# Two mixing layers: the spatial mixer's projection is issued between the differential heads' projection and their turning

## The chip, the cores and the metric

The kernel runs on one core of one Trainium2 chip. The metric is the device time of one launch in microseconds (us). Engines are named as in the profile: PE is TensorE (PEld its weight loads), DVE is VectorE, ACT is ScalarE, POOL is GpSimd, SP is the engine that here only issues DMAs. Each engine takes its instructions strictly in the order in which they were queued.

## The reference, cut to what matters

Two blocks on a sequence of 256 rows of 1024 values: first a block with a gated delta rule, latent attention and two SwiGLU layers, then a second block with two layers `l`. Only the second block is touched. In each of its layers four mixers run on the same normed `h` and their 256-wide results are put side by side:

```
pa, pb, pc, pd = split(h @ w_in[l], GROUP_COLS)
ya = rwkv7_mixer(pa, ...)            # a scan over the rows, chunked
yb = diff_attention_mixer(pb, ...)   # q, k: norm per head, rotary turn; two softmaxes
yc = spatial_gating_mixer(pc, ...)   # u, v = split(gelu(pc)); v = layer_norm(v); u * (w @ v + b)
yd = forgetting_attention(pd, ...)   # q, k: norm per head; softmax with a decay
x = x + g1 * (concat(ya, yb, yc, yd) @ w_out[l])
```

All matrices are f32. A product of f32 accuracy is made of three matmuls of a 32-bit form whose operands are a high part and a low remainder: high by high, low by high, high by low.

## The kernel before, in words

`mix2` (L1424) is one mixing layer; it runs twice, near 790 to 965 us and near 1182 to 1365 us of the profiled span. The 256 rows are two halves `t` of 128 rows.

**Weights.** `weights` (L446) loads one chunk of weights by a DMA on SP into one of three raw slots, casts it to its high part on ACT (L464) and takes the low remainder on POOL (L467) or on DVE (L469). Which of the two is said by the letter, P or V, at the chunk's running number in the string `w` of the stage's plan (L68 to L98). The high and low parts go to one of three slots (`WSB`); a slot is free again when the last matmul that reads it is done. A chunk of `w_b` or `w_d` has 768 columns, one of `w_c` or `w_out` has 1024.

**The parts.** `mix2` names its parts by letters and `order` lists them. `b2+L` weaves two parts, two steps of the first to one of the second; what stands after `/` runs once the tiles for the result exist.

- B, `diff_heads` (L1899): projection of the differential heads (`proj_qkv`, L1874, 8 chunks, 96 matmuls into two PSUM banks `ps_qk` and one `ps_v`), then, for each half `t`, the turning: squares on ACT, a norm on DVE (`head_scale`), the rotary turn of q on DVE and of k on POOL (L1937 to L1943, six products each), four transposes on PE (L1947), and copies to `at_q` and `b_kbd` on ACT and DVE (L1949 to L1955).
- V, `rwkv_values`; L, `rwkv_levels`; S, `rwkv_scan`; s, `rwkv_out`: the scan mixer. V is a chain over PE, ACT and POOL; L joins the inverse of 32-row blocks that `tri_inverse` (L1858) makes on DVE; S walks over the two chunks of 128 rows.
- M, `forget_gates`; D, `forget_heads` (8 chunks, 96 matmuls, then the norm of the heads and transposes); d, `forget_attend`.
- b, `diff_attend`; e, `diff_out`.
- C, `spatial_in` (L2143): 4 chunks, 48 matmuls of 512 columns into two PSUM banks `ps_c`, for each chunk first one half and then the other; then for each half Gelu on ACT straight from PSUM (L2161, L2164) and the layer norm (L2165 to L2174). c, `spatial_out`, uses it.

Before the change the order is `B V M b2+L D+S C / e s d c`. Last comes `proj_out`, the output projection `ps_o`.

**What sets the order on an engine.** The order in the source is a priority, not the queue: a planner walks through the program in a modelled time and gives each engine the earliest listed instruction whose inputs the model holds ready. So a late part's work is found early in the trace wherever its inputs are there and an engine was modelled idle, and a matmul of a later projection stands between the links of an earlier chain. Tiles of one tag share a fixed number of buffers: tag `acc` (the projections) has 4 PSUM banks, tags `mm` and `A` (the small products) 2 each. `issue_after` puts a block's instructions behind a given instruction on that engine.

Of the kernel before, what the change touches and what calls it, by code (L numbers as in the profile page):

```python
# [11 lines left out]
F32 = mybir.dt.float32  # L12
F32R = mybir.dt.float32r
I32 = mybir.dt.int32
AF = mybir.ActivationFunctionType
# [5 lines left out]
D = 1024  # L21
S = 256
# [4 lines left out]
CW = 1024  # L27
# [25 lines left out]
        w='PPVVVPVVPPPPVPPVPVVVVPVVVP',  # L53
# [14 lines left out]
    m0=dict(  # L68
        np=80,
        w='PPPVVPPPVPPPPVPPPVVPPVPPVVVVPVVVVPP',  # L70
        order='B V M b2+L D+S C / e s d c',
        out=(2, 3, 0, 1, 6, 7, 4, 5),
        hold=4,
        nb=(0,),
# [10 lines left out]
    m1=dict(  # L85
        np=60,
        w='PPPPPPPPPPPVVPVPPVVVVVVVVVVPVVVVVVP',
        order='B V M b2+L D+S C / e s d c',
        out=(2, 3, 0, 1, 6, 7, 4, 5),
        hold=4,  # L90
        nb=(0, 1),
# [288 lines left out]
class Prog:  # L380
# [105 lines left out]
    def mm3_b(self, ps, lhs, w, sl, start, stop, shared=False):  # L486

        nc = self.nc
        wh, wl = w
        xh, xl = lhs  # L490
        kw = dict(skip_group_check=True) if shared else {}
        nc.tensor.matmul(ps, xh, wh[:, sl], start=start, stop=False, **kw)  # L492
        nc.tensor.matmul(ps, xl, wh[:, sl], start=False, stop=False, **kw)  # L493
        nc.tensor.matmul(ps, xh, wl[:, sl], start=False, stop=stop, **kw)  # L494

    def rsqrt(self, out, src, shape, scale, eps, pool=None, tag=None, bufs=1, key=""):

# [926 lines left out]
    def mix2(self, x, l):  # L1424
        nc, tc, ap = self.nc, self.tc, self.ap
        self.lay = self.xp.tile([128, LAYER.n], F32, name=f"lay{l}", tag="lay")
        with tc.issue_after(self.last_raw.ins):
            nc.sync.dma_start(self.lay, ap[f"layer{l}"])
        with ExitStack() as st:
            self.psum(st, 2)  # L1430
            self.rows = self.next_mod
            self.prefetch(*((ap[f"w_k{l}"][c], 776) for c in range(3)))
            self.mq = st.enter_context(tc.tile_pool(name=f"mixq{l}", bufs=1, reuse_waits="tile"))
            xn = [self.mq.tile([128, D], F32, name="xn", tag="b_p", bufs=2) for _ in range(2)]
            sp = self.mq.tile([128, 2, CW], F32R, name="w_sp", tag="b_kbd")
            self.spare = [lambda: (sp[:, 0], sp[:, 1])]
            mp = st.enter_context(tc.tile_pool(name=f"mix{l}", bufs=1, reuse_waits="tile"))
            dr = st.enter_context(tc.tile_pool(name=f"mixd{l}", bufs=1, space=DRAM))
            hl, norm = self.norm_steps(x, True, lambda t: xn[t])
            gate = self.gate_row(2, mp)  # L1440
            A = self.rwkv_scores(l, hl, norm, mp, dr)
            B, C, Dd = {}, {}, {}
            G = dict(B=lambda: self.diff_heads(l, hl, mp, B), C=lambda: self.spatial_in(l, hl, mp, C), D=lambda: self.forget_heads(l, hl, mp, Dd), M=lambda: self.forget_gates(mp, dr, A["f"], Dd, A["last_exp"]),
                     V=lambda: self.rwkv_values(mp, A), L=lambda: self.rwkv_levels(mp, A), S=lambda: self.rwkv_scan(l, mp, A), s=lambda: self.rwkv_out(mp, A, yh, yl),
                     b=lambda: self.diff_attend(l, mp, B), e=lambda: self.diff_out(mp, B, yh, yl), c=lambda: self.spatial_out(l, mp, C, yh, yl), d=lambda: self.forget_attend(l, mp, Dd))
# [451 lines left out]
    def diff_heads(self, l, hl, mp, res):  # L1897
# [21 lines left out]
                V.tensor_tensor(tab[:, t, i], gn[:, :, g], cs[:, c, t].unsqueeze(1).to_broadcast([128, 2, 16]), op=ALU.mult)  # L1919
        ps, pv = yield from self.proj_qkv(hl, ap[f"w_b{l}"])  # L1920
        v = mp.tile([128, 2, 256], F32, name="at_v", tag="at_v", bufs=2)
        qT = mp.tile([128, 2, S], F32, name="at_q", tag="at_q", bufs=2)
        for t in range(2):
            if t == 0:
                nc.scalar.copy(v, pv)
            xn = mp.tile([128, 16, 32], F32, name="b_xn", tag="b_xn", bufs=2)
            rs = self.head_scale(xn, ps[t], 16, 32, 1e-6)
            pv4 = ps[t].rearrange("p (q h d) -> p q h d", q=2, h=8)
# [14 lines left out]
                E.tensor_tensor(ro[:, q, :, 1], ro[:, q, :, 1], m, op=ALU.add)  # L1943
            rf = ro.rearrange("p q h s f -> p (q h s f)")
            pt = self.pm.tile([128, 4, 128], F32, name="ps_qk", tag="mm")
            for j in range(4):
                nc.tensor.transpose(pt[:, j], rf[:, j * 128 : j * 128 + 128], self.ident)  # L1947
            tk = slice(t * 128, t * 128 + 128)
            nc.scalar.copy(qT[:, :, tk], pt[:, 0:2])  # L1949
            for q in range(4):  # L1950
# [6 lines left out]
        res.update(v=v, qT=qT, kbd=kbd, nlam=nlam)  # L1957

    def diff_attend(self, l, mp, a):
        nc = self.nc  # L1960
# [182 lines left out]
    def spatial_in(self, l, hl, mp, res):  # L2143
# [3 lines left out]
        nc.sync.dma_start(sw, ap[f"sgw{l}"])  # L2147
        nc.gpsimd.affine_select(sw, sw, [[0, 4], [1, 128]], ALU.is_ge, 0.0, base=0, channel_multiplier=-1)
        ps = [self.pa.tile([128, 512], F32, name="ps_c", tag="acc") for _ in range(2)]
        for k in range(8):  # L2150
            if k % 2 == 0:
                w = self.weights(ap[f"w_c{l}"][k // 2], CW)
            for t in range(2):
                tk = slice(t * 128, t * 128 + 128)
                self.mm3_b(ps[t], (hl[0][:, k, tk], hl[1][:, k, tk]), w, slice(512 * (k % 2), 512 * (k % 2) + 512), k == 0, k == 7)
            if k % 2:
                yield
        u = mp.tile([128, 2, 256], F32, name="c_u")
        vn = mp.tile([128, 4, 2, 64], F32, name="c_v")
        for t in range(2):  # L2160
            nc.scalar.activation(u[:, t], ps[t][:, 0:256], AF.Gelu)  # L2161
            v = mp.tile([128, 256], F32, name="c_v0", tag="c_v0", bufs=2)
            s = self.sm.tile([128, 2], F32, name="c_s", tag="c_s")
            nc.scalar.activation(v, ps[t][:, 256:512], AF.Gelu, accum_out=s[:, 0:1])  # L2164
            V.tensor_scalar(s[:, 0:1], s[:, 0:1], 1.0 / 256, None, op0=ALU.mult)  # L2165
            V.tensor_scalar(v, v, s[:, 0:1], None, op0=ALU.subtract)
            v2 = mp.tile([128, 256], F32, name="c_v2", tag="c_v0", bufs=2)
# [7 lines left out]
        res.update(sw=sw, u=u, vn=vn)  # L2175

    def spatial_out(self, l, mp, a, yh, yl):
        nc = self.nc
# [93 lines left out]
```

## Time and profile before

| | us |
|---|---|
| three timed runs | 1557.66, 1558.67, 1561.19 (median 1558.67) |
| the profiled execution | 1570.74 |
| its span, first to last instruction | 1569.0 |
| PE busy in the span | 1455.1 (93%) |
| DVE busy | 1120.2 (71%) |
| ACT busy | 811.7 (52%) |
| POOL busy | 659.3 (42%) |
| granted PE clock, mean of the span | 0.972 of full |

Busy time of PE is that of pipelined matmuls, so a PE that is busy all the time need not be at its peak. An idle time in brackets stands ahead of the instruction that ended it, with what it had waited for. A granted clock of 1.00 in a stretch is 2.4 GHz, of 0.50 it is 1.2 GHz.

### The profile page before, as it was taken

The numbers are of one execution on the slowest core, as the hardware profiler recorded it, in microseconds if no ns is written. First come the engines' busy times: TensorE is split into PE (matmuls) and PEld (weight loads), VectorE is DVE, ScalarE is ACT, GpSimd is POOL, SyncE is SP. The second block draws the span as 40 slices with busy tenths as digits, with TensorE's granted clock in tenths as the row PEclk, the third lists the DMA queues.
The fourth block names the chain that finished last, engine by engine and source line by source line (L and its number), as shares of the span: only waits on it lengthen the run. The fifth ranks groups of instructions, "written<-read, shape, count | busy, mean of one in ns | idle before, by whom it ended". The sixth has DMA issues, their size and how long they took to land. (4 is left out here: it accounts for less than half of the span.)

```text
span 1569.0 us, 25783 instructions
## 1 busy us (share of the span) xinstructions
PE 1455.1 (93%) x9586; PEld 1286.3 (82%) x9586; DVE 1120.2 (71%) x2352; ACT 811.7 (52%) x1474; POOL 659.3 (42%) x433
## 2 busy tenths in 40 slices
PE   5999989899999899999988988998998899899998
PEld 4998878699988788999877766898987776589987
DVE  3588668778686577887477597788876768766752
ACT  4676545544543464554354665455544465466651
POOL 3577623256452522443136312465644622236530
PEclk9999999999999999999998999999999999999999
DMA  4756622677884455988434325576773442465551
GB/s 159 232 167 189 182 69 68 209 289 281 298 306 131 136 182 188 337 313 311 170 115 128 108 78 184 203 285 252 264 247 126 120 130 72 141 202 180 191 188 38
DMA packets 103246, 292.96 MB, mean 187 GB/s; under 512 B 28072, under 2 KB 37968, under 8 KB 96976
## 3 DMA queue, kind: packets, MB, share of 16 engines
q1 hardware_dynamic: 93872, 237.12, 44.9%
q10 hardware_dynamic: 8896, 53.14, 9.2%
q8 instruction: 75, 1.23, 0.3%
q0 software_dynamic: 352, 1.06, 0.2%
q14 instruction: 51, 0.42, 0.1%
HBM read 288.04 MB, written 3.24 MB: 186 GB/s over the span
## 5 line engine op out<-in xcount | busy, mean ns | idle before, releaser
L467 POOL TENSOR_TENSOR wl<-raw,wh 128x1024 fp32r<-128x1024 f32 (+4 forms) x162 | 405.6, 2511 | 414.6 <-ACT wh L464 350.7
L464 ACT CAST wh<-raw 128x1024 fp32r<-128x1024 f32 (+3 forms) x421 | 424.1, 1018 | 249.1 <-PE ps_o L493 97.4
L469 DVE TENSOR_TENSOR wl<-raw,wh 128x1024 fp32r<-128x1024 f32 (+2 forms) x259 | 356.9, 1385 | 145.2 <-ACT wh L464 143.2
L480 PE MATMUL ps_gu<-h_hi,wh 128*128 128x256 f32 x1280 | 313.1, 283 | 6.9 <-DVE gu_u L2226 6.3
L480 PE MATMUL ps_gu<-h_lo,wh 128*128 128x256 f32 x1280 | 312.7, 283 | 0.0
L480 PEld LDWEIGHTS ps_gu<-h_hi,wh 128*128 128x128 f32 x1280 | 244.9, 191 | 7.6 <-issue 6.7
L480 PEld LDWEIGHTS ps_gu<-h_lo,wh 128*128 128x128 f32 x1280 | 245.0, 191 | 0.1
L1394 DVE CUSTOM_DVE_ANT_0 ada_raw<-ada_raw,ada_cond 128x1024 f32<-128x1024 f32 x96 | 160.5, 1685 | 68.7 <-DMA ada_raw<-in_ada 68.7
L483 PE MATMUL ps_gu<-h_hi,wl 128*128 128x256 f32 x1280 | 179.2, 283 | 5.9 <-DVE wl L469 3.9
L483 PEld LDWEIGHTS ps_gu<-h_hi,wl 128*128 128x128 f32 x1280 | 164.4, 192 | 6.5 <-DVE wl L469 4.1
L494 PE MATMUL ps_o<-wl,act_h 128*128 128x512 f32 x352 | 138.8, 394 | 0.0
L493 PE MATMUL ps_o<-wh,act_l 128*128 128x512 f32 x352 | 138.6, 394 | 0.0
L492 PE MATMUL ps_o<-wh,act_h 128*128 128x512 f32 x352 | 138.3, 393 | 0.0
L2226 DVE SCALAR_TENSOR_TENSOR gu_u<-ps_gu,f2s,gu_u 128x254 f32<-128x254 f32 (+1 forms) x176 | 82.0, 477 | 40.7 <-ACT gu_u L2224 38.6
L738 POOL TENSOR_TENSOR act_l<-gu_t,act_h 128x256 fp32r<-128x256 f32 x44 | 51.8, 1179 | 102.7 <-ACT act_h L737 102.7
L2229 POOL TENSOR_TENSOR gu_t<-gu_t,gu_u 128x256 f32<-128x256 f32 x44 | 47.4, 1078 | 97.4 <-DVE gu_u L2226 84.1
L494 PEld LDWEIGHTS ps_o<-wl,act_h 128*128 128x128 f32 x352 | 66.1, 188 | 15.4 <-issue 0.5
L493 PEld LDWEIGHTS ps_o<-wh,act_l 128*128 128x128 f32 x352 | 66.1, 188 | 15.1 <-issue 0.2
L492 PEld LDWEIGHTS ps_o<-wh,act_h 128*128 128x128 f32 x352 | 66.1, 188 | 15.0 <-issue 0.2
L737 ACT CAST act_h<-gu_t 128x256 fp32r<-128x256 f32 x44 | 17.7, 407 | 95.8 <-DVE gu_t L736 95.8
L480 PE MATMUL ps_g<-h_hi,wh 128*128 128x256 f32 x256 | 66.5, 294 | 0.0
L480 PE MATMUL ps_g<-h_lo,wh 128*128 128x256 f32 x256 | 66.2, 293 | 0.0
(662 smaller groups left out, 2978.1 us busy)
## 6 DMA issues: line engine op xcount, KB each, us to landing
ada_raw<-in_ada ACTq DMA_DIRECT2D x48, 1024.0 KB, 6.2
raw<-in_f_gu SPq DMA_DIRECT2D x88, 512.0 KB, 5.4
raw<-in_u_gu SPq DMA_DIRECT2D x88, 512.0 KB, 4.2
raw<-in_f_dn SPq DMA_DIRECT2D x44, 512.0 KB, 6.2
raw<-in_u_dn SPq DMA_DIRECT2D x44, 512.0 KB, 4.3
raw<-in_g_qkv SPq DMA_DIRECT2D x32, 512.0 KB, 3.5
raw<-in_g_z SPq DMA_DIRECT2D x16, 512.0 KB, 5.7
raw<-in_g_out SPq DMA_DIRECT2D x16, 512.0 KB, 3.7
```

Source lines behind the costliest of these rows:

```text
L464: self.last_copy = nc.scalar.copy(wh[:, :cols], raw[:, :cols])
L467: nc.gpsimd.tensor_tensor(wl[:, :cols], raw[:, :cols], wh[:, :cols].bitcast(F32), op=ALU.subtract)
L469: nc.vector.tensor_tensor(wl[:, :cols], raw[:, :cols], wh[:, :cols].bitcast(F32), op=ALU.subtract)
L480: nc.tensor.matmul(ps, wh[:, k * width + m0 : k * width + m0 + m], xx[:, k, :], start=(n == 0), stop=(n == last))
L483: self.last_mm = nc.tensor.matmul(ps, wl[:, k * width + m0 : k * width + m0 + m], xh[:, k, :], start=False, stop=(n == last))
L492: nc.tensor.matmul(ps, xh, wh[:, sl], start=start, stop=False, **kw)
L493: nc.tensor.matmul(ps, xl, wh[:, sl], start=False, stop=False, **kw)
L494: nc.tensor.matmul(ps, xh, wl[:, sl], start=False, stop=stop, **kw)
L738: nc.gpsimd.tensor_tensor(al[:, m, :], t, ah[:, m, :].bitcast(F32), op=ALU.subtract)
L1394: nc.vector.tensor_tensor_reduce(raw[:, j], raw[:, j], self.cond, 1.0, 0.0, op0=ALU.mult, op1=ALU.add, accum_out=mod[:, i : i + 1])
L2226: nc.vector.scalar_tensor_tensor(u[:, j, d:], ps[:, j, : S - d], cw[:, 3 * q + 2 - d : 3 * q + 3 - d], u[:, j, d:], op0=ALU.mult, op1=ALU.add)
L2229: nc.gpsimd.tensor_tensor(t, t, u[:, 0], op=ALU.mult)
```

## The change

The letter H is new: `diff_turn` holds the turning that was the second half of B. The letter G is new: `spatial_gelu` holds the Gelu and the layer norm that were the end of C. The order becomes `B C H V M b2+L D+S G / e s d c` in both layers. In C the 48 matmuls go by pairs of chunks: two chunks are held, and each half runs its 24 matmuls of the pair in one go of 12 and 12. At the end of C four copies on ACT take the projection out of PSUM, to `c_u` and `c_v0`; Gelu then works in SBUF, in place. The transposes of the turning are put behind the last matmul of C by `issue_after`. The strings of letters stay, so C's chunks now take the numbers 16 to 19 and D's the numbers 20 to 27 (before: 24 to 27 and 16 to 23). In the first layer those letters are `PVVPPVPP` and `VVVV`, in the second `PVVVVVVV` and `VVVP`.

```diff
-        order='B V M b2+L D+S C / e s d c',
+        order='B C H V M b2+L D+S G / e s d c',          # in m0 and in m1
...
-        nc.tensor.matmul(ps, xh, wl[:, sl], start=False, stop=stop, **kw)
+        self.last_mm = nc.tensor.matmul(ps, xh, wl[:, sl], start=False, stop=stop, **kw)
...
+            G = dict(H=lambda: self.diff_turn(l, mp, B, C), G=lambda: self.spatial_gelu(mp, C), ...
...
         ps, pv = yield from self.proj_qkv(hl, ap[f"w_b{l}"])
         v = mp.tile([128, 2, 256], F32, name="at_v", tag="at_v", bufs=2)
+        nc.scalar.copy(v, pv)
+        res.update(v=v, kbd=kbd, nlam=nlam, tab=tab, ps=ps)
+
+    def diff_turn(self, l, mp, res, behind):
...
         for t in range(2):
-            if t == 0:
-                nc.scalar.copy(v, pv)
...
-            for j in range(4):
-                nc.tensor.transpose(pt[:, j], rf[:, j * 128 : j * 128 + 128], self.ident)
+            with self.tc.issue_after(behind["mm"].ins):
+                for j in range(4):
+                    nc.tensor.transpose(pt[:, j], rf[:, j * 128 : j * 128 + 128], self.ident)
...
-        for k in range(8):
-            if k % 2 == 0:
-                w = self.weights(ap[f"w_c{l}"][k // 2], CW)
+        for c in range(0, 4, 2):
+            w = [self.weights(ap[f"w_c{l}"][c + i], CW) for i in range(2)]
             for t in range(2):
                 tk = slice(t * 128, t * 128 + 128)
-                self.mm3_b(ps[t], (hl[0][:, k, tk], hl[1][:, k, tk]), w, slice(512 * (k % 2), 512 * (k % 2) + 512), k == 0, k == 7)
-            if k % 2:
-                yield
+                for k in range(2 * c, 2 * c + 4):
+                    self.mm3_b(ps[t], (hl[0][:, k, tk], hl[1][:, k, tk]), w[k // 2 - c], slice(512 * (k % 2), 512 * (k % 2) + 512), k == 0, k == 7)
+            yield
         u = mp.tile([128, 2, 256], F32, name="c_u")
+        v = [mp.tile([128, 256], F32, name="c_v0", tag="c_v0", bufs=3) for _ in range(2)]
+        for t in range(2):
+            nc.scalar.copy(v[t], ps[t][:, 256:512])
+            nc.scalar.copy(u[:, t], ps[t][:, 0:256])
+        res.update(mm=self.last_mm, sw=sw, u=u, v=v)
+
+    def spatial_gelu(self, mp, res):
...
-            nc.scalar.activation(u[:, t], ps[t][:, 0:256], AF.Gelu)
+            nc.scalar.activation(u[:, t], u[:, t], AF.Gelu)
...
-            nc.scalar.activation(v, ps[t][:, 256:512], AF.Gelu, accum_out=s[:, 0:1])
+            nc.scalar.activation(v, v, AF.Gelu, accum_out=s[:, 0:1])
```

## Rows read from the trace of the kernel before

**Rows 1.** Stretches: from:to, length, busy PE PEld DVE ACT POOL, clock, DMA
```profile
851.60:866.40 14.80, 11.14 (x49) 8.73 (x48) 13.43 (x75) 5.23 (x9) 7.98 (x14) 0.77 0.24 77
866.40:887.80 21.40, 20.47 (x115) 15.14 (x114) 8.71 (x21) 11.75 (x25) 10.03 (x15) 1.00 0.57 172
908.00:919.30 11.30, 11.30 (x73) 9.10 (x72) 11.04 (x44) 6.98 (x19) 2.27 (x2) 1.00 0.15 49
1245.10:1258.70 13.60, 9.98 (x48) 7.96 (x47) 13.51 (x75) 5.23 (x9) 5.25 (x12) 0.87 0.29 86
```
**Rows 2.** Timeline of PE around the turning: start, length, what, idle before
```profile
858.98 1.13 PE L1947 MATMUL ps_qk<-ident,b_ro 128*128 128x128 f32 x4 [3.59 <-DVE b_ro L1943]
866.88 0.60 PE L1661 MATMUL ps_vt<-ident,a_v 128*128 128x128 f32 x4
1252.49 0.89 PE L1947 MATMUL ps_qk<-ident,b_ro 128*128 128x128 f32 x4 [3.61 <-DVE b_ro L1943]
1259.17 0.60 PE L1661 MATMUL ps_vt<-ident,a_v 128*128 128x128 f32 x4
```
**Rows 3.** Timeline of DVE, first layer, around the turning
```profile
859.33 0.95 DVE L469 TENSOR_TENSOR wl<-raw,wh 128x768 fp32r<-128x768 f32 x1
864.29 0.29 DVE L1943 TENSOR_TENSOR b_ro<-b_ro,ps_qk 128x128 f32<-128x128 f32 x1
871.11 0.42 DVE L1634 COPY a_AT<-ps_ti 128x256 f32<-128x256 f32 x1
```
**Rows 4.** Matmuls into ps_c, both layers: durations, first and last start
```profile
L492 PE MATMUL ps_c<-wh,h_hi x32: 388/393/581, 896.1 to 1316.7; 128*128 128x512 f32 x32
```
**Rows 5.** A stretch, instructions of ps_c alone: busy PE PEld ACT, clock
```profile
923.10:927.00 3.90, 3.90 (x18) 3.02 (x17) 0.00 (x0) 1.00 0.10 41
```
**Rows 6.** Timeline of ACT, first layer
```profile
860.15 0.37 ACT L1949 COPY at_q<-ps_qk 128x256 f32<-128x256 f32 x1 [6.92 <-PE ps_qk L1947]
892.13 1.28 ACT L1982 ACT_TABLE_LOAD   x1
893.43 0.40 ACT L1982 ACTIVATE b_p<-b_p,b_mx 128x128 f32<-128x128 f32 x1
...
934.85 1.28 ACT L2117 ACT_TABLE_LOAD   x1
```
**Rows 7.** Instructions on tile c_w: the one on POOL, both layers
```profile
L2148 POOL TENSOR_SCALAR_AFFINE_SELECT c_w<-c_w x2: 637/860/1082, 803.7 to 1191.0; 128x512 f32<-128x512 f32 x2
```
**Rows 8.** A stretch right after the inverse; columns as in Rows 1
```profile
871.60:883.50 11.90, 11.30 (x61) 7.90 (x60) 1.48 (x1) 5.73 (x13) 7.09 (x14) 1.00 0.47 124
```
**Rows 9.** DVE's costliest groups from 929.4 to 941.4 us, two of the layer norm's
```profile
L517 DVE SCALAR_TENSOR_TENSOR rs_t<-rs_h,rs_s 128x1 f32<-128x1 f32 x6 | 1.3, 216 | 0.1
...
L2171 DVE SCALAR_TENSOR_TENSOR c_v<-c_v,c_rs,lay 128x256 f32<-128x256 f32 x2 | 1.0, 481 | 0.0
```
**Rows 10.** A stretch, instructions of wl alone: busy PE PEld DVE POOL, clock
```profile
895.00:930.00 35.00, 7.30 (x18) 3.40 (x18) 3.64 (x3) 2.62 (x1) 1.00 0.21 66
```
**Rows 11.** Timeline of DVE in the scan, first layer
```profile
914.07 1.21 DVE L469 TENSOR_TENSOR wl<-raw,wh 128x1024 fp32r<-128x1024 f32 x1
...
918.30 2.35 DVE L521 SCALAR_TENSOR_TENSOR rs_s<-rs_t,rs_s 128x4 f32<-128x4 f32 x1
...
920.64 0.28 DVE L1826 TENSOR_TENSOR a_Y<-ps_y,a_GR 128x128 f32<-128x128 f32 x1
```
**Rows 12.** Timeline of POOL, first layer
```profile
856.60 0.46 POOL L1938 TENSOR_TENSOR b_ro<-b_xn,b_tab 128x128 f32<-128x128 f32 x1 [6.27 <-DVE a_stmp L1871]
...
918.01 2.62 POOL L467 TENSOR_TENSOR wl<-raw,wh 128x1024 fp32r<-128x1024 f32 x1 [3.96 <-PE ps_c L494]
```
**Rows 13.** Stretches behind waits of PE; columns as in Rows 1
```profile
859.70:864.50 4.80, 4.80 (x14) 3.83 (x14) 4.54 (x21) 2.77 (x5) 3.46 (x7) 0.50 0.28 84
...
1321.80:1325.60 3.80, 3.80 (x13) 2.92 (x12) 3.80 (x22) 1.02 (x4) 0.00 (x0) 0.55 0.30 103
```
**Rows 14.** Timeline of PE, second layer, the wait ahead of the second stretch
```profile
1321.11 0.50 PE L493 MATMUL ps_o<-wh,yl 128*128 128x512 f32 x1 [1.09 <-DVE yl L1475]
```

More of the change, by code (lines that the diff above doesn't have):

```diff
@@ L87 @@
         w='PPPPPPPPPPPVVPVPPVVVVVVVVVVPVVVVVVP',
-        order='B V M b2+L D+S C / e s d c',
+        order='B C H V M b2+L D+S G / e s d c',
         out=(2, 3, 0, 1, 6, 7, 4, 5),
@@ L1442, in mix2 @@
             B, C, Dd = {}, {}, {}
-            G = dict(B=lambda: self.diff_heads(l, hl, mp, B), C=lambda: self.spatial_in(l, hl, mp, C), D=lambda: self.forget_heads(l, hl, mp, Dd), M=lambda: self.forget_gates(mp, dr, A["f"], Dd, A["last_exp"]),
+            G = dict(H=lambda: self.diff_turn(l, mp, B, C), G=lambda: self.spatial_gelu(mp, C), B=lambda: self.diff_heads(l, hl, mp, B), C=lambda: self.spatial_in(l, hl, mp, C), D=lambda: self.forget_heads(l, hl, mp, Dd), M=lambda: self.forget_gates(mp, dr, A["f"], Dd, A["last_exp"]),
                      V=lambda: self.rwkv_values(mp, A), L=lambda: self.rwkv_levels(mp, A), S=lambda: self.rwkv_scan(l, mp, A), s=lambda: self.rwkv_out(mp, A, yh, yl),
@@ L1921, in diff_heads @@
         v = mp.tile([128, 2, 256], F32, name="at_v", tag="at_v", bufs=2)
+        nc.scalar.copy(v, pv)
+        res.update(v=v, kbd=kbd, nlam=nlam, tab=tab, ps=ps)
+    def diff_turn(self, l, mp, res, behind):
+        nc = self.nc
+        V = nc.vector
+        kbd, tab, ps = (res[k] for k in "kbd tab ps".split())
         qT = mp.tile([128, 2, S], F32, name="at_q", tag="at_q", bufs=2)
+        res.update(qT=qT)
         for t in range(2):
-            if t == 0:
-                nc.scalar.copy(v, pv)
             xn = mp.tile([128, 16, 32], F32, name="b_xn", tag="b_xn", bufs=2)
@@ L1956, in diff_heads @@
             yield
-        res.update(v=v, qT=qT, kbd=kbd, nlam=nlam)
     def diff_attend(self, l, mp, a):
@@ L2149, in spatial_in @@
         ps = [self.pa.tile([128, 512], F32, name="ps_c", tag="acc") for _ in range(2)]
-        for k in range(8):
-            if k % 2 == 0:
-                w = self.weights(ap[f"w_c{l}"][k // 2], CW)
+        for c in range(0, 4, 2):
+            w = [self.weights(ap[f"w_c{l}"][c + i], CW) for i in range(2)]
             for t in range(2):
                 tk = slice(t * 128, t * 128 + 128)
-                self.mm3_b(ps[t], (hl[0][:, k, tk], hl[1][:, k, tk]), w, slice(512 * (k % 2), 512 * (k % 2) + 512), k == 0, k == 7)
-            if k % 2:
-                yield
+                for k in range(2 * c, 2 * c + 4):
+                    self.mm3_b(ps[t], (hl[0][:, k, tk], hl[1][:, k, tk]), w[k // 2 - c], slice(512 * (k % 2), 512 * (k % 2) + 512), k == 0, k == 7)
+            yield
         u = mp.tile([128, 2, 256], F32, name="c_u")
+        v = [mp.tile([128, 256], F32, name="c_v0", tag="c_v0", bufs=3) for _ in range(2)]
[4 more added lines that the diff above has]
+    def spatial_gelu(self, mp, res):
+        nc = self.nc
+        V = nc.vector
+        u = res["u"]
         vn = mp.tile([128, 4, 2, 64], F32, name="c_v")
         for t in range(2):
-            nc.scalar.activation(u[:, t], ps[t][:, 0:256], AF.Gelu)
-            v = mp.tile([128, 256], F32, name="c_v0", tag="c_v0", bufs=2)
+            nc.scalar.activation(u[:, t], u[:, t], AF.Gelu)
+            v = res["v"][t]
             s = self.sm.tile([128, 2], F32, name="c_s", tag="c_s")
-            nc.scalar.activation(v, ps[t][:, 256:512], AF.Gelu, accum_out=s[:, 0:1])
+            nc.scalar.activation(v, v, AF.Gelu, accum_out=s[:, 0:1])
             V.tensor_scalar(s[:, 0:1], s[:, 0:1], 1.0 / 256, None, op0=ALU.mult)
             V.tensor_scalar(v, v, s[:, 0:1], None, op0=ALU.subtract)
-            v2 = mp.tile([128, 256], F32, name="c_v2", tag="c_v0", bufs=2)
+            v2 = mp.tile([128, 256], F32, name="c_v2", tag="c_v0", bufs=3)
             nc.scalar.activation(v2, v, AF.Square, accum_out=s[:, 1:2])
@@ L2174, in spatial_in @@
             nc.gpsimd.tensor_tensor(vn[:, :, t], v.rearrange("p (g c) -> p g c", g=4), self.lcol("sglnb").rearrange("p (g c) -> p g c", g=4), op=ALU.add)
-        res.update(sw=sw, u=u, vn=vn)
+        res.update(vn=vn)
     def spatial_out(self, l, mp, a, yh, yl):
```

## The prediction

> **What bounds the kernel now.** The page comes first: PE is busy for 93% of the span, which says that elsewhere, in the feed-forward stages, PE sets the pace; the change touches only the two mixing layers. So the next view is the busy time by stretches inside a layer. The reader is to see that the limit changes along it. While the differential heads are turned, DVE is busy 13.43 us of 14.80 and PE only 11.14, at a mean granted clock of 0.77; the second layer has the same picture, 13.51 us of DVE in 13.60 [rows 1]. While the scan mixer's values are made (V), PE is busy 20.47 us of 21.40 and DVE 8.71. In the scan both are full: 11.30 and 11.04 us of 11.30.
>
> The timeline of PE then shows the hole at which the change aims: ahead of the first transposes of the turning PE waits 3.59 us in the first layer and 3.61 us in the second, both times for the last rotary product on DVE [rows 2]. Behind the first wait the granted clock was 0.50, the lower of the two levels, for 4.80 us [rows 13]. Is the hole on the path? The timeline of DVE says mostly not. V's first transposes start at 866.88 us, 7.9 us after the hole has ended [rows 2], because they come behind the transposes of the second half, whose last rotary product ended on DVE at 864.58 us (864.29 + 0.29) [rows 3]. The inverse that the levels of the scan need ends on DVE too, at 871.53 us [rows 3]. PE in the hole lacks work; what everything waits for is DVE.
>
> **The change, part by part.**
>
> *C's matmuls move into the hole.* There are 96 / 2 = 48 a layer (three lines of 32 for two layers [rows 4]); at full clock 17 to 18 of them fit into 3.90 us [rows 5], 0.22 to 0.23 us each, so C takes some 10.8 us, from 851.6 to 862.4 us. The first half's transposes, now behind C's last matmul, go from 859.0 to 862.4 us; that is still before the second half is turned (864.58 us), so V's start stays where it is. What changes in front of V is DVE's load: the low parts taken there are now of 1024 columns (1.21 us [rows 11]) instead of 768 (0.95 us [rows 3]), and by the letters it is two of them in the first layer and three in the second where two of D's stood. That is 2 x 0.26 = 0.5 us and 3 x 1.21 - 2 x 0.95 = 1.7 us. Against it stands that V started 2.3 us after its last input (866.88 - 864.58), behind filling matmuls; of this I give back 0.6 us a layer. Value: -0.1 and +1.1, together +1.0 us. Ends: -2.3 a layer, if all of that gap goes, and +4, which is the first rival.
>
> *D's matmuls take C's old place* between the links of b, L and S. D has 96 matmuls before and after, so PE's work is the same; 3.6 us of waiting a layer is filled and taken off somewhere later, where PE is not what ends last. I take 0 for it; the end below is the second rival.
>
> *Four copies out of PSUM*, of the size of the 0.37 us copy [rows 6]: 1.5 us of ACT a layer, in the 6.92 us that ACT waited for the turning's transposes. Nothing; 1.5 us a layer if that cover were gone.
>
> *Gelu and the layer norm* keep their place in the source, but not, I expect, in the trace: their input is in SBUF at 864 us instead of in PSUM at 927. A part listed as late as C had its mask on POOL done at 803.7 us, as soon as its data were there [rows 7]; the planner should pull G forward alike, into the stretch after the inverse, where DVE is busy 1.48 us of 11.90 and ACT 5.73 [rows 8]. What leaves the tail is 24 DVE instructions; the two largest groups are 1.3 and 1.0 us [rows 9], the other sixteen have 0.15 to 0.35 us each, in all some 5 us, which by their starts hold DVE for 3.5 us because short ones overlap. They stand between the scan's last norm and the forgetting attention, where DVE runs without a pause. Two thirds on the path, 2.3 us a layer: -4.6 us. Ends: 0, if G is not pulled forward (third rival), and the whole 5.1 plus one table load, -6.4 us a layer. Behind the turning ACT loads a table three times a layer now, for b's Exp, for Gelu and for d's Exp (the first and the last stand in [rows 6]); with Gelu ahead of b it is two. I count the load within the two thirds, since DVE and not ACT was late there.
>
> The Trainium skill, "ScalarE: Activation LUTs", section "What ACT_TABLE_LOAD costs", puts a switch at 2.66 us, load and drain together. Here the load takes 1.28 us and the first Exp starts 0.02 us behind it [rows 6], so the trace bears out the load alone. By the page's figure the end of this term would be 1.4 us a layer lower and the sum the same.
>
> *Weight conversions shift.* From 895 to 930 us DVE takes three low parts, 3.64 us, and POOL one, 2.62 us [rows 10]. Two of DVE's are C's, and the first of them, at 914.07 us, is followed by a scan product that starts only at 920.64 us [rows 11]; beside POOL's, which began at 918.01 us [rows 12], a DVE instruction on 128x4 values took 2.35 us [rows 11]. With C gone the chunks in that stretch are D's last, shorter by 0.26 us, and the output projection's first, which find their slots free earlier. The same work falls earlier, upon b and L, which also need DVE. Value: -1.0 us a layer, -2.0 us; ends, worked out from one of 1.21 us each way and the 2.35 us: -3.6 and +2.4 a layer.
>
> *The scan loses its filler.* PE had C's 48 matmuls between the scan's links up to 927 us; now D's will be used up some 10 us sooner. Then PE waits more often, and the granted clock can fall: it did in the second layer after waits of about 1 us [rows 14], to 0.55 for 3.80 us [rows 13]. A stretch of 4.80 us at 0.50 costs 2.4 us of full-clock work, of which the links of a chain are the smaller part: +0.6 us a layer, +1.2 us. Ends: 0 and +4.5 (fourth rival). The holes of 3.6 us with their low clock vanish, but only for filling matmuls.
>
> The Trainium skill, "TensorE: Matmul & The Clock Gate", section "Why this matters for your kernels", advises to leave TensorE no long idle gaps between bursts, because the clock then goes back to its lower level. It speaks for the filled hole and against the emptied scan; where it would decide is the fourth rival.
>
> Sum: +1.0 + 0 + 0 - 4.6 - 2.0 + 1.2 = -4.4 us. The profiled execution took 1570.74 us, a span of 1569.0 and 1.74 us around it; it would take 1566.3. It lies 12.1 us (0.8%) above the median of 1558.67; a difference of a few us is carried over unscaled: 1554.3 us, with a range of its own from 1551 to 1557.
>
> **The rivals.**
>
> *First, slower: C's fourth chunk comes late and holds the turning.* With three slots it can be cast only after 18 of the first pair's 24 matmuls, near 855.9 us; its low half then falls to POOL in the first layer (letter P), up to 2.62 us [rows 12], beside the k half's six rotary products of 0.46 us. If it queues behind these it is there near 862.4 us, 16 matmuls are left, and C ends near 866 us: past 864.6 us, from which point it decides. The transposes then hold V, and DVE's copies behind them hold the inverse. Price: near 4 us in a layer (in the second the chunk falls to a full DVE), 1554.3 + 8 = 1562.3 us. Against it: C's chunks are listed ahead of the turning and should be given the engine first.
>
> *Second: the hole is on the path after all,* since PE is busy 96% of V and all of the scan [rows 1]: 3.59 + 3.61 us of waiting and twice 2.4 us of low clock, 12.0 us, come off whole: 1546.7 us. Against it stands DVE's chain ahead of V.
>
> *Third: no change.* G is not pulled forward, or what it leaves is taken up by D's norm, which moves later into the same DVE: +1.0 - 2.0 + 1.2 = +0.2 us, 1558.9 us. The change would then fill a hole that nobody waits at.
>
> *Fourth, slower: the scan on the low clock.* Some nine links of groups of matmuls, each longer by near 0.5 us, 4.5 us a layer in place of 0.6: 1554.3 + 7.8 = 1562.1 us. This is the rule of the clock gate at work; the 1.00 that the first layer shows in its scan, beside waits of 1 to 2 us, speaks against it, the second layer's 0.55 for it.
>
> **How the numbers follow.** Forecast 0.42, first rival 0.15, second 0.13, third 0.22, fourth 0.08. A measurement of this kernel can tell about 0.2%, 3.1 us. Faster by more than that (below 1555.6): 0.83 of the forecast's own range and the second rival, 0.35 + 0.13 = 0.48. Within it: 0.17 of the forecast and most of the third, 0.27. Slower: the first and fourth and a rest, 0.25. The range takes in the second rival's and the slow rivals' inner halves: 1547 to 1562.
>
> **What would show it.** Right: no wait of PE between the end of B's matmuls and the turning's transposes, a granted clock of 1.00 there, V's first transposes within 1.5 us of where they were after B's end; Gelu and its table load near 865 us after scaling to the start of the layer, two loads a layer from there on; the output projection's last matmuls 2 to 3 us earlier. Wrong: Gelu still behind the scan; a wait for `wl` inside C's matmuls; V's start later by 2 us or more; a stretch of the scan at 0.50; a layer shorter by 6 us or more.

## The result, and the profile after

The changed kernel took 1581.35 us (median of 4, 1576.11 to 1585.94), the kernel before 1559.93 us beside it (4 runs, 1557.66 to 1566.25): a ratio of 1.0105, 95% interval 1.0069 to 1.0142, about 16 us slower. (The two medians are 21.4 us apart; in what follows the ratio is used, for the experiments too.) The forecast was 1554.3 us and the range ended at 1562.

The profiled execution after took 1577.36 us, the one before 1570.74, and the stages outside the mixing layers, which the change does not touch, were some 15 us shorter in it. So the layers are compared by themselves here, and totals by the ratio only. A layer runs from its first matmul into `ps_lk` to the end of its last one into `ps_o` from `w_sp`. The first layer grew from 167.4 to 180.8 us, the second from 176.7 to 184.7: 21.4 us together. All starts below are from timelines of PE. *Front* is B's first matmul to V's first transposes; *behind V* is the rest of the layer from there; the *scan* in it is b's first scores (`ps_bs`) to d's first (`ps_ds`).

| us | front | behind V | of it scan | layer |
|---|---|---|---|---|
| before, first / second layer | 32.1 / 30.9 | 96.3 / 103.9 | 46.2 / 51.9 | 167.4 / 176.7 |
| after | 39.3 / 37.1 | 104.1 / 104.0 | 52.5 / 53.8 | 180.8 / 184.7 |

The second layer lost in the front alone (+6.3, and 1.6 ahead of B); the first lost 7.2 in the front and 7.9 behind V, and was 1.7 shorter ahead of B. First the page, then stretches of the changed kernel: B's end to V's start in both layers, which answer to those of [rows 1], and two stretches of the first scan.

```profile
span 1575.7 us, 25797 instructions
PE 1455.2 (92%) x9586; PEld 1286.2 (82%) x9586; DVE 1132.2 (72%) x2352; ACT 810.8 (51%) x1480; POOL 666.7 (42%) x433
```
```profile
844.10:866.10 22.00, 19.62 (x88) 15.74 (x87) 19.95 (x79) 12.97 (x25) 13.84 (x16) 0.92 0.48 145
1249.00:1268.90 19.90, 17.58 (x86) 14.07 (x84) 18.02 (x83) 11.95 (x23) 6.02 (x12) 1.00 0.41 126
888.60:913.50 24.90, 20.11 (x159) 14.47 (x159) 20.14 (x95) 14.06 (x41) 2.44 (x1) 0.87 0.07 23
913.50:926.30 12.80, 9.46 (x56) 8.44 (x55) 10.19 (x43) 6.10 (x18) 1.30 (x2) 0.77 0.26 82
```
The first column after the comma is PE, the third DVE. The turning took 22.0 us where it took 14.8, and DVE worked 19.95 of them instead of 13.43. PE's clock there rose from 0.77 to 0.92, and PE was busy 8 us longer; V came later all the same.

PE's timeline in the turning, answering to [rows 2]: C's last matmul, the first half's transposes, V's first ones; in the second layer a matmul of D, the first half's transposes, the last two of the second half, and V's first.

```profile
855.48 0.39 PE L494 MATMUL ps_c<-wl,h_hi 128*128 128x512 f32 x1
858.34 0.85 PE L1955 MATMUL ps_qk<-ident,b_ro 128*128 128x128 f32 x4 [2.02 <-DVE b_ro L1950]
866.61 0.60 PE L1661 MATMUL ps_vt<-ident,a_v 128*128 128x128 f32 x4
...
1261.15 0.39 PE L492 MATMUL ps_v<-wh,h_hi 128*128 128x256 f32 x1 [0.65 <-ACT c_u L2168]
1261.50 0.60 PE L1955 MATMUL ps_qk<-ident,b_ro 128*128 128x128 f32 x4
...
1268.92 0.64 PE L1955 MATMUL ps_qk<-ident,b_ro 128*128 128x128 f32 x2 [0.84 <-POOL b_ro L1950]
1269.35 1.06 PE L1661 MATMUL ps_vt<-ident,a_v 128*128 128x128 f32 x4
```
C was done 2.5 us before the transposes in the first layer, and they still waited 2.02 us for DVE. In the second layer the last transposes waited for POOL's product of k as well. Now DVE itself in the first layer, answering to [rows 3], and below it POOL's row of the same time and one of ACT's:

```profile
844.36 1.23 DVE L469 TENSOR_TENSOR wl<-raw,wh 128x1024 fp32r<-128x1024 f32 x1 [0.92 <-ACT wh L464]
845.63 0.68 DVE L1892 TENSOR_REDUCE hn_s<-b_xn 128x16 f32<-128x512 f32 x1
847.36 1.23 DVE L469 TENSOR_TENSOR wl<-raw,wh 128x1024 fp32r<-128x1024 f32 x1
849.55 2.36 DVE L521 SCALAR_TENSOR_TENSOR rs_s<-rs_t,rs_s 128x16 f32<-128x16 f32 x1
852.05 1.68 DVE L519 TENSOR_TENSOR rs_t<-rs_s 128x16 f32<-128x16 f32 x1
858.65 0.94 DVE L469 TENSOR_TENSOR wl<-raw,wh 128x768 fp32r<-128x768 f32 x1
863.00 0.42 DVE L1963 COPY b_kbd<-ps_qk 32x256 f32<-32x256 f32 x1 [1.61 <-ACT b_kbd L1961]
864.97 0.29 DVE L1950 TENSOR_TENSOR b_ro<-b_ro,ps_qk 128x128 f32<-128x128 f32 x1
```
```profile
849.48 4.22 POOL L467 TENSOR_TENSOR wl<-raw,wh 128x1024 fp32r<-128x1024 f32 x2 [5.58 <-ACT wh L464]
...
861.75 0.83 ACT L464 CAST wh<-raw 128x768 fp32r<-128x768 f32 x1 [1.53 <-POOL b_ro L1945]
```
From B's end to the last rotary product it was 12.98 us before and is 21.16 now. The 8.2 us more can be read from these rows: the norm's sums, behind C's first low part, start 1.53 us behind B's end and not 0.12 ahead of it (1.65); C's second low part (1.23); two steps of the norm on 128x16 values that take 2.36 and 1.68 us instead of 0.17 (3.7); and a wait for ACT (1.61). The two long steps lie on POOL's two low parts (C's last, D's first) and end with them. What DVE waited for on ACT, a copy to `b_kbd`, stood behind a cast of D's weights for which ACT had waited itself. V starts 1.35 us behind the last product instead of 2.30, so 7.2 us are left. In the second layer three of C's low parts are on DVE:

```profile
1248.04 1.48 DVE L469 TENSOR_TENSOR wl<-raw,wh 128x1024 fp32r<-128x1024 f32 x1 [0.55 <-ACT wh L464]
1251.09 1.21 DVE L469 TENSOR_TENSOR wl<-raw,wh 128x1024 fp32r<-128x1024 f32 x1
1254.18 1.23 DVE L469 TENSOR_TENSOR wl<-raw,wh 128x1024 fp32r<-128x1024 f32 x1 [0.74 <-ACT wh L464]
1260.61 0.95 DVE L469 TENSOR_TENSOR wl<-raw,wh 128x768 fp32r<-128x768 f32 x1
1263.08 0.94 DVE L469 TENSOR_TENSOR wl<-raw,wh 128x768 fp32r<-128x768 f32 x1
```
The last two are D's, and of D's there was one between the halves before. C's chunks are used up by C's matmuls within the turning, their slots come free, and D's chunks are made in the same stretch as well. On ACT Gelu was pulled forward, and two table loads are left from the turning on:

```profile
853.83 1.28 ACT L2180 ACT_TABLE_LOAD   x1
...
889.11 1.28 ACT L1989 ACT_TABLE_LOAD   x1
```

### The profile page after: what moved, and what is told of

It reads as the page before. It is cut to its first block, busy times and chain, and to the rows that moved or that the text cites. A ratio compares the mean times of both kernels' runs of the same rounds, so it can differ in the third digit from the quotient of the medians.

```text
span 1575.7 us, 25797 instructions
## 1 busy us (share of the span) xinstructions
PE 1455.2 (92%) x9586; PEld 1286.2 (82%) x9586; DVE 1132.2 (72%) x2352; ACT 810.8 (51%) x1480; POOL 666.7 (42%) x433
## 3 DMA queue, kind: packets, MB, share of 16 engines
q8 instruction: 75, 1.23, 0.3%
## 4 chain that ended last, share of the span: by engine, by line
PE 55%; DVE 15%; ACT 4%; issue 4%; DMA 3%; POOL 2%; SPq 0%; POOLq 0%; ACTq 0%; DVEq 0%
PE ps_gu L480 15%; PE ps_gu L483 7%; PE ps_o L492 6%; PE ps_o L493 6%; PE ps_o L494 6%; DVE wl L469 3%; ACT wh L464 1%; DVE gu_u L2242 1%; DVE ada_raw L1394 1%; DMA raw<-in_u_gu 1%; DMA ada_raw<-in_ada 1%; POOL wl L467 1%; PE ps_u L480 1%; PE ps_bs L1982 1%; DVE rs_t L519 1%
## 5 line engine op out<-in xcount | busy, mean ns | idle before, releaser
L469 DVE TENSOR_TENSOR wl<-raw,wh 128x1024 fp32r<-128x1024 f32 (+2 forms) x259 | 351.6, 1365 | 128.0 <-ACT wh L464 126.7
L1394 DVE CUSTOM_DVE_ANT_0 ada_raw<-ada_raw,ada_cond 128x1024 f32<-128x1024 f32 x96 | 175.6, 1844 | 56.8 <-DMA ada_raw<-in_ada 56.8
```

Of the source, the lines that this page charges most:

```text
L469: nc.vector.tensor_tensor(wl[:, :cols], raw[:, :cols], wh[:, :cols].bitcast(F32), op=ALU.subtract)
L1394: nc.vector.tensor_tensor_reduce(raw[:, j], raw[:, j], self.cond, 1.0, 0.0, op0=ALU.mult, op1=ALU.add, accum_out=mod[:, i : i + 1])
```

## The experiments

Theory F: C's low parts, on DVE or on POOL in DVE's way, lengthen the turning, and the layer with it. Rivals: C's matmuls or the held transposes (P), the scan without filler on the lower clock (S), Gelu in the turning (G). Layer stages are from each run's own profile, as above; "front" and so on give the first and the second layer.

**e5_no_low**: F's main test. In `weights`, for C's chunks alone:
```diff
-            wl = pw[0].tile([128, CW], F32R, name="wl", tag="wl", bufs=pw[1])
+            wl = pw[0].tile(...) if low is None else low   # C: low = part of hl[1]
...
+        if low is not None:
+            return wh, wl
```


> The changed kernel with only the low parts of C's weights left out (C's third product reads other data in SBUF); loads, casts on ACT and all 48 matmuls stay. Theory F, narrowed to the low parts on DVE and POOL: the front comes down from 39.3 and 37.1 to 33 to 35 us in the first and 32 to 33.5 us in the second layer, all that leaving the weights out altogether gave (32.4 and 32.4). Rival (the casts on ACT, 1.05 us each, or the loads delay the turning): it stays at 36 us or more. Total 1.004 to 1.008 by F.

Ratio to before 1.0015 (0.9999 to 1.0032): without its low parts, the changed kernel is 14 us faster, more than F expected. Front 32.2 / 32.4, behind V 98.0 / 103.1, layers 169.2 / 179.0. PE's timeline, B's first matmul and V's first transposes:
```profile
835.19 0.40 PE L494 MATMUL ps_qk<-wh,h_hi 128*128 128x512 f32 x1
...
867.44 0.66 PE L1663 MATMUL ps_vt<-ident,a_v 128*128 128x128 f32 x4 [0.22 <-ACT b_kbd L1963]
```
All 48 matmuls of C stand ahead of the transposes here, with their casts and loads, and V starts as early as before. So P falls as what delays V, and so does the gain from the hole: with it filled neither front nor layer is shorter. (Holding the transposes is not quite free: DVE waited 0.83 / 2.22 us here for the copies behind them, while fewer of D's low parts fell into the turning.)

**e2_noweights_new and e2_noweights_old**: C's weights left out altogether, in the changed and in the old order.
```diff
-            w = [self.weights(ap[f"w_c{l}"][c + i], CW) for i in range(2)]
+            w = [[x[:, 0:4].rearrange("p k s -> p (k s)") for x in hl] for i in range(2)]
```


> The changed kernel with C's weights left out: its 48 matmuls a layer stay where they are but read data that are in SBUF anyway, so that C's four loads, casts and low parts a layer are gone; the other conversions keep their engines. To be set against e2_noweights_old. Theory F (C's conversions in the turning are what delays V): from B's first matmul to V's first transposes 39.3 and 37.2 us in the changed kernel come down to 32 to 34 in both layers, within 2 us of e2_noweights_old. Rival P (C's matmuls themselves, or the transposes being held behind them, delay V): 37 us or more, 5 us over e2_noweights_old. Total: by F 4 to 12 us over e2_noweights_old (what is left is the scan), by P 18 us or more.

> The kernel before with C's weights left out in the same way, its matmuls in their old place in the scan. From B's first matmul to V's first transposes 31 to 33 us in both layers by every theory, as before (32.1 and 30.9). The total is faster than before by what C's eight conversions cost there: by theory 2 to 8 us, a ratio of 0.995 to 0.999; if they cost nothing, 1.000.

New: 1.0054 (1.0034 to 1.0073), front 32.4 / 32.4. Old: 1.0012 (0.9995 to 1.0030), front 32.6 / 31.0. The front again falls to the old length. The total does not fall as far as in e5_no_low, though loads and casts are gone as well: behind V the first layer took 105.3 us. So the fronts are what the low parts cost, and of e5_no_low's 14 us the part behind V cannot be put down to them. The old order gains nothing from four loads and eight conversions less; no price of theirs is seen where they stood.

**e8_extra_low**: the opposite direction, the kernel before with the suspected work added in its turning (`n` is 4, then 2).
```diff
...
+            for i in range(n):
+                self.nc.vector.tensor_tensor(low, hl[0][:, 0:2]..., junk..., op=ALU.subtract)
         ss = self.sm.tile([128, nh], F32, name="hn_s", tag=f"hn_s{nh}")
```


> The kernel before, C in its old place, with six more subtractions of 128x512 a layer on DVE ahead of the turning's norm (four ahead of the first half's sums, two ahead of the second's), of two inputs in SBUF, like the low part of a weight; nothing reads their results. About 0.65 us each, 3.9 us a layer. Theory F (the turning is DVE's, and what DVE does there is paid one for one): from B's first matmul to V's first transposes 32.1 and 30.9 become 35 to 37 in both layers, and the total grows by 6 to 9 us, 1.004 to 1.006. Rival (the front's delay is taken up later, and the changed kernel is slow because of its order behind V): the total grows by less than 3 us, 1.002 or less.

1.0095 (1.0073 to 1.0117), 15 us slower, with C in its old place. The added instructions (the tile's row: count, then least, middle and longest duration in ns) and PE's wait for the turning:
```profile
L1895 DVE TENSOR_TENSOR x_low<-h_hi,b_xn x12: 679/681/687, 853.1 to 1261.2; 128x512 fp32r<-128x512 f32 x12
```
```profile
864.59 1.15 PE L1952 MATMUL ps_qk<-ident,b_ro 128*128 128x128 f32 x4 [8.17 <-DVE b_ro L1948]
...
872.95 0.60 PE L1661 MATMUL ps_vt<-ident,a_v 128*128 128x128 f32 x4
```
Six times 0.68 us are 4.1 us of DVE a layer; the front became 37.9 / 35.5, +5.8 / +4.6, somewhat more than one for one. In the second layer that is nearly all (behind V 103.8). In the first 9.2 us more were lost behind V (105.5), though nothing there was changed in the source.

**e4_low_on_dve and e10_d_on_dve**: letters. e4: C's are VVVV in both layers; e10: in the first layer D's and the first of the output projection's are V.

> The changed kernel with all four low parts of C's weights a layer on DVE (before one or two of them were on POOL). Theory L (in the first layer DVE lost 3.7 us of the turning because a POOL low part held it: 2.36 and 1.68 us in two of the short steps of the norm): the front of the first layer (B's first matmul to V's first transposes) comes down from 39.3 to 37.5 us or so (two more low parts of 1.23 us on DVE, one of the two blocks gone), and the second layer's goes up from 37.1 by one low part, to 38.0. Rival (a POOL low part costs DVE nothing, those two steps were late for another reason): the first layer goes up by 2.5 us, to 41.8. Total: 1.008 to 1.012 by L.

> The changed kernel with the first layer's letters changed: D's eight low parts and the output projection's first one all on DVE (three and one of them were on POOL). The second layer is as changed. Theory (a POOL low part holds DVE while it runs: 1.68 us in the turning, 1.8 us ahead of b's first scores): the first layer's front falls from 39.3 to 38 us, the step from b's first to its second scores from 5.2 to 3.7 us, the layer from 180.8 to 176 to 178 us; total 1.007 to 1.010. Rival (DVE is full there and the four low parts cost it what the blocks did): 180 to 182 us and 1.010 to 1.012.

e4: 1.0131 (1.0112 to 1.0150), front 39.1 / 35.2; neither number came. In the first layer DVE did about what L said: one hold went (of 2.36 us), two low parts of 1.23 came, one of them ahead of B's end, and DVE's last product stood 19.5 us behind B's end instead of 21.2. But now V waited for POOL, whose products of k stood behind two low parts of D:
```profile
860.19 4.47 POOL L467 TENSOR_TENSOR wl<-raw,wh 128x768 fp32r<-128x768 f32 x2
```
```profile
868.09 0.44 PE L1955 MATMUL ps_qk<-ident,b_ro 128*128 128x128 f32 x2 [1.52 <-POOL b_ro L1950]
```
So low parts on either engine can set V's start, since the turning runs over both. In the second layer the front fell by 2 us with one low part more on DVE. e10: 1.0071 (1.0048 to 1.0094), front 36.5 / 37.2, first layer 176.0, as the hold theory had it: of the 13.4 us that this layer lost, 4.8 went with POOL's four low parts (2.8 in the front, 3.5 behind V, and 1.6 lost ahead of B, where nothing was changed). The second layer, whose code is that of the changed kernel, took 184.7 us in both.

**e1_filler, e3_late_gelu, e7_late_filler, e6_all_three**: the scan and Gelu. The filler is 48 matmuls on data in SBUF behind D's last; the late Gelu is
```diff
+            with self.tc.issue_after(self.last_y2.ins):
                 nc.scalar.activation(u[:, t], u[:, t], AF.Gelu)
```
with `last_y2` the squares of the scan's second half (L1838); e6 has both, and no weights for C.

> The changed kernel with 48 more matmuls of 128x512 a layer, on data that are there anyway and into PSUM that nobody reads, placed behind D's last matmul, where C stood before; no weights, no DMA, no conversion with them. Theory S (the scan lost its filler and runs at the lower clock): the granted clock is 1.00 through the scan again, the stretch from b's first scores to d's first scores in the first layer comes down from 52.6 us to about 48, in spite of some 10.8 us more of PE work; the whole is 2 to 8 us faster than the changed kernel, a ratio to before of 1.005 to 1.009. Rival (PE's work counts there): both layers get longer, by up to 10 us each, a ratio of 1.015 to 1.023. If the scan's loss is the order of DVE's instructions and not the clock: same as the changed kernel, 1.010, with the clock at 1.00.

> The changed kernel with only Gelu and what follows it held back to where it ran before, behind the second half's squares of the scan's norm on ACT. Theory (pulling Gelu forward is worth a little in the tail and costs a little in the turning): within 4 us of the changed kernel, a ratio to before of 1.008 to 1.013, with the tail (d's first scores to the last output matmul) back from 26.7 to 29 us or more in the second layer and the front shorter by 1 to 2 us. Rival G (Gelu, its table load and the layer norm in the turning are what costs): 8 us or more faster than the changed kernel, 1.005 or less, and V starts 5 us earlier. By the prediction's own term (4.6 us gained by pulling it forward) it would be 4 us slower, 1.013.

> The changed kernel with its weights, with Gelu held back and with the 48 filling matmuls in the scan: what is left against before should be the front. Theory: the front stays at 39 to 40 and 37 us (+7 and +6), the scan is at most 2 us longer than before (46.2 and 51.9) at a clock of 1.00; total +12 to +16 us, 1.008 to 1.010. Rival (the layers' length is set by all engines' work together, so that what leaves one place comes back at the next): 1.011 or more, as each of the two alone.

> Three things at once: the changed kernel with C's weights left out, Gelu held back behind the scan's squares, and 48 matmuls of filling in the scan. If conversions, Gelu's place and the lost filler are all there is, the mixing layers are as long as those of e2_noweights_old (169.4 and 177.9 us) within 3 us, in spite of 10.8 us more of PE work in each, and the total is 1.001 to 1.004. If the order of D's projection behind C (D ends 10 to 12 us later) costs by itself, the layers stay longer by 4 us or more each and the total is 1.006 or more.

e1: 1.0097 (1.0075 to 1.0119). The clock is full through the scan, as these stretches of the first layer show, and the scan is 2.0 / 1.5 us shorter (50.5 / 52.3), no more:
```profile
893.10:918.00 24.90, 23.30 (x181) 17.24 (x182) 19.04 (x95) 14.27 (x41) 2.44 (x1) 1.00 0.07 23
918.00:929.00 11.00, 10.75 (x73) 8.93 (x72) 10.64 (x41) 5.90 (x17) 1.73 (x2) 1.00 0.29 95
```
e3: 1.0115 (1.0094 to 1.0137), as the changed kernel: scan and V's stage are 5.1 / 7.4 us shorter, the tail (d's first scores to the layer's end) 4.2 / 5.7 longer. What the tail gains by Gelu's forward place, scan and V's stage lose; by which step is not shown, since Gelu and its norm are done ahead of the scan. G falls, as the front (39.9 / 37.1) did not move. e7: 1.0056 (1.0036 to 1.0075), better than expected, front 39.3 / 37.3 unmoved, scan 46.3 / 48.9. e6: 1.0017 (1.0003 to 1.0030), layers 180.0 / 175.4 against 169.4 / 177.9: right in the total, not layer by layer.

So filler and late Gelu, which each alone changed nothing that the total shows, together brought it down, with C's weights (1.0105 to 1.0056) and without them (1.0054 in e2_noweights_new to 1.0017 in e6); the two layers together became 4.3 and 2.6 us shorter. A part of the loss is theirs, then, and not the low parts'.

**e11_c_first**: the order `C B H V M b2+L D+S G`.

> The changed kernel with C one place further forward, ahead of B's projection, so that its loads, casts and low parts come in the scores stage instead of in the turning. Theory F: the front falls from 39.3 and 37.1 to 31 to 33 us in both layers, the stage ahead of B grows from 38 and 43 by 4 to 9 us (10.8 us of matmuls into a stage in which PE is busy 31 of 37 us), total 1.002 to 1.007. Rival (C's early place is bad because it takes the filler from the scan, wherever its conversions are): 1.010 or more.

1.0132 (1.0105 to 1.0159). The front fell to 35.6 / 34.4 only, and not to 31 to 33, so F missed here: in the first layer the norm's sums start 4.8 us behind B's end, behind a low part of D. The stage ahead of B grew to 53.0 / 54.2 us, by 14 / 12 and not 4 to 9: ahead of B, C's 48 matmuls do not hide. But here the scan has no filler either, and it took 45.0 / 45.2 us, less than before, at clocks of 0.92 and 0.84 in its second parts:
```profile
928.00:949.40 21.40, 15.77 (x87) 11.52 (x86) 19.42 (x85) 10.45 (x25) 4.71 (x7) 0.92 0.15 49
...
1333.00:1354.70 21.70, 16.21 (x81) 12.37 (x80) 18.55 (x82) 7.99 (x21) 4.67 (x7) 0.84 0.07 26
```
So S falls as the main reason: no filler and a lower clock do not by themselves make a long scan. The shortest scan of all, e4's in the first layer (43.8 us), had a mean clock of 0.90.

**e12_hold_low**: the kernel before with less DVE work in its turning.
```diff
+            with self.tc.issue_after(after.ins) if after else ExitStack():   # D's chunks from the third on
                 nc.vector.tensor_tensor(wl[:, :cols], raw[:, :cols], wh[:, :cols].bitcast(F32), op=ALU.subtract)
```


> The kernel before, C in its old place, with the one low part of D's weights a layer that ran on DVE between the turning's halves (0.95 us) held back behind the last rotary product of the second half. Theory F the other way round: the front falls by about 1 us in both layers, to 31 and 30, what DVE did not do there is gained and D's matmuls, one chunk later, still end long before the scan; total 1 to 4 us faster, 0.997 to 1.000. Rival (PE misses the filling matmuls of that chunk more than DVE misses the microsecond): V's stage gets longer by as much or more, 1.000 to 1.003.

1.0054 (1.0032 to 1.0075), slower. The front did fall, to 29.9 / 30.2:
```profile
831.84 0.40 PE L493 MATMUL ps_qk<-wh,h_hi 128*128 128x512 f32 x1
...
861.75 0.62 PE L1662 MATMUL ps_vt<-ident,a_v 128*128 128x128 f32 x4
```
but behind V it took 105.4 / 108.8, with D's projection ending 8 / 6 us later. V's start is a limit of the layer, not the only one.

**e13_old_all_dve, e14_new_all_dve, e15_old_no_low**: what is lost behind V in the first layer. e13 and e14 have the same letters, V from C's or D's first chunk to the end of the layer; e15 leaves C's low parts out in the old order.

> The kernel before with every low part from C's or D's first on to the end of the layer on DVE in both layers, so that no POOL low part can hold DVE there. To be set against e14_new_all_dve. DVE gets eight and two more low parts, of which the holds give back some: total 0 to 6 us slower than before, 1.000 to 1.004; from V's first transposes to the end of the first layer 96 to 100 us.

> The changed kernel with every low part from C's first on to the end of the layer on DVE, the same letters as e13_old_all_dve. Theory H (what the first layer lost behind V, 7.9 us, is the holds of DVE by POOL low parts falling in other places): behind V the first layer takes as long as in e13_old_all_dve within 2 us, and the two kernels differ by the fronts alone, 5 to 7 us a layer less what the tail gained, total 1.004 to 1.009 times before. Rival O (it is the order behind V, a changed list of short DVE steps, whoever makes the low parts): the first layer stays 5 us or more longer behind V than e13_old_all_dve; total 1.009 or more.

> The kernel before with only the low parts of C's weights left out; the fourth corner to before, after and e5_no_low. Theory F (C's low parts cost little in the scan and 17 us of the layers in the turning): within 3 us of before, 0.998 to 1.001, as with the weights left out altogether (1.0012), so that without low parts the change costs 1.0015 less that. If C's low parts cost as much in their old place, this is 8 us or more faster, 0.995 or less, and the move of C costs as much without them.

e13: 1.0030 (1.0013 to 1.0046), first layer behind V 97.5 (second layer 183.0, longer than before). e14: 1.0109 (1.0088 to 1.0130), 102.7, front 35.8 / 35.2. With no POOL low part anywhere, 5.2 us of the 7.9 are still there, so holds are the smaller part of it, as e10 had it too (100.6). e15: 1.0056 (1.0035 to 1.0077): less work, and slower; the front stayed (33.2 / 31.6), behind V the first layer took 106.4. So the four corners do not add up in the total: low parts left out, -14 us in the changed kernel, +9 in the old one. In the front F holds: -7.1 / -4.7 against +1.1 / +0.7.

What stays open: over all 17 kernels the first layer took 96 to 109 us behind V. Kernels with C in its old place have both ends (96.3 before, 97.5, 97.9, and 105.4, 105.5, 106.4), those with C moved too (96.2, 98.0, and up to 108.6). Equal code repeated to 0.1 us in e10's second layer, but not everywhere: the stage ahead of B in the first layer, with PE's order the same in all kernels but e11, took 37.3 to 40.2 us, and the granted clock, third from the end of each row, went with it (before, after and e3):
```profile
795.80:834.80 39.00, 32.70 (x208) 29.82 (x207) 31.34 (x87) 23.03 (x45) 17.14 (x11) 0.96 0.39 124
...
790.00:827.30 37.30, 31.01 (x206) 28.45 (x206) 30.11 (x84) 22.88 (x45) 16.45 (x11) 1.00 0.40 126
...
791.10:830.50 39.40, 33.94 (x207) 31.36 (x205) 30.04 (x83) 22.68 (x45) 16.48 (x11) 0.91 0.37 120
```
Behind V the clock goes with the length too; these rows are the first layer before and after, columns as in [rows 1].
```profile
866.90:963.20 96.30, 89.11 (x546) 67.33 (x545) 71.82 (x282) 61.54 (x150) 28.85 (x29) 1.00 0.33 104
...
866.60:970.70 104.10, 87.89 (x507) 66.05 (x506) 71.33 (x278) 54.85 (x139) 25.36 (x26) 0.92 0.27 82
```
First layers with a mean clock of 0.96 or more behind V took 96 to 101 us (e1, with its filler, 103), those at 0.95 or less 102 to 109. Whether the clock made them long, or the waits of a long layer brought the clock down, is not shown. The kernel before, at 1.00 throughout, is at the good end of that scatter, and nearly every edit left it; which of the short steps decides was not found.

## Why the prediction was wrong

- **C's matmuls move into the hole** is the step that failed. It valued the turning's change at +1.0 us for both layers, with +4 a layer as the outer end; it measured +7.2 and +6.3. DVE's load was priced as an exchange, two or three of C's low parts "where two of D's stood". One of D's stayed in the first layer and both in the second, so that C's came mostly on top: three and five low parts on DVE where there had been two. It also left out what [rows 11] had shown for the scan, that a POOL low part can hold a short DVE step for 2.35 us: here 2.36 and 1.68 us, in the middle of the chain that V waits for. The prediction had itself read that DVE was busy 13.43 of 14.80 us there [rows 1]; on an engine that full, added work had to be counted whole. That it is the low parts, e5_no_low and e2_noweights_new show (fronts back to 32.2 to 32.4) and e8_extra_low from the other side.
- **D as filler, 0**, could not be told apart. In e12 D ended 8 us later and V's gain was lost, but in e5_no_low it ended 11 us later and the first layer lost only 1.7 us behind V.
- **The four copies, 0**: not quite. In the second layer a matmul of D waited 0.65 us for the last of them (1261.15 us), and the transposes stood behind it. The 1.61 us for which DVE waited for ACT in the first layer came behind a cast, not behind the copies.
- **Gelu, -4.6**: pulled forward with two table loads as forecast, but worth nothing that the total shows: tail +0.5 / -3.8 us, and in e3 scan and V's stage gave back what the tail lost.
- **Conversions, -2.0**: 0 within the interval where C's stood (e2_noweights_old, 1.0012).
- **The scan's filler, +1.2**: the clock fell (0.87 and 0.77 in the first layer), and e1 puts filler and full clock together at 2.0 and 1.5 us of scan. In the total that is not seen by itself, only together with the late Gelu (e7, e6).
- The sum took the stretch behind V as fixed but for these terms. In the first layer it grew by 7.9 us. Without POOL's low parts 3.5 (e10) or 1.4 (e14) of them went, with filler and late Gelu 3.6 (e7); these are not known to add up, and the cause stays open.
- **First rival** (1562.3): V late, as it said, but by another cause: C ended 2.5 us ahead of the transposes (its wait for a low part was 0.36 us), so no late chunk held them, and its price of 4 us a layer was too low. **Second** falls (e5: the hole filled, front and layer no shorter), and with it the **third**'s last sentence holds: nobody waited at that hole. **Fourth**: the low clock came; what e1 finds for clock and filler is 2.0 and 1.5 us, not 4.5 a layer, and e11's scan was short without either.

## What to carry to other kernels

A matmul that is moved takes its weights' conversions with it: before it fills a hole of PE, look at which engine makes its operands and how full that engine is in the new place. If the hole exists because DVE is late, work that needs DVE lengthens it. And in a schedule that was fitted to its own timings, expect any edit to cost some microseconds elsewhere, and test the stage for itself before the total is believed.

## What the hardware showed

A POOL low part held some DVE instructions until its end and others not at all. These rows of the kernel before are POOL, and DVE in the same time:
```profile
846.68 3.65 POOL L467 TENSOR_TENSOR wl<-raw,wh 128x768 fp32r<-128x768 f32 x2 [0.43 <-ACT wh L464]
```
```profile
847.43 0.22 DVE L1872 TENSOR_TENSOR ps_ti<-ps_ti,a_stmp 128x52 f32<-128x52 f32 x1
```
The inverse's steps, with an operand in PSUM, ran at 0.22 us beside it; the norm's steps with both operands in SBUF took 2.36 and 1.68 us instead of 0.17. It goes the other way too: in the second layer of the changed kernel POOL's last product of k, for which V's start waited, took 1.21 us instead of 0.46 beside a low part on DVE.
```profile
1267.60 0.95 DVE L469 TENSOR_TENSOR wl<-raw,wh 128x768 fp32r<-128x768 f32 x1
```
```profile
1267.65 1.21 POOL L1950 TENSOR_TENSOR b_ro<-b_ro,b_m 128x128 f32<-128x128 f32 x1
```
The Trainium skill, "SBUF — State Buffer", section "SBUF: two separate sides", states such a rule: DVE and GpSimd share a pair of SBUF ports as an exclusive lock for a whole instruction, which a DVE instruction with two SBUF inputs needs. The trace agrees. Two inputs are not the only case: in e10 a step with one SBUF input, 128x16, took 2.38 us beside a POOL low part (857.61 us). With four such low parts moved to DVE, e10's first layer was 4.8 us shorter.
